# Attention's product with V in single precision, two heads on the two column halves

## The chip, the cores and the metric

The kernel runs on one core of one Trainium2 chip. The metric is the device time of one execution in microseconds (us). Lower is better.

## The reference: what is computed

A trunk of two layers works on a residual stream of 512 positions by 1024 features in float32. Each layer is a SwiGLU feed-forward half-step, a mixer of parallel attention heads, a second feed-forward half-step, and a gated input embedding, with layer norms between. The change is in the mixer, which has three kinds of heads of width 64, all causal over 512 positions:

```python
# 4 "nsa" heads share one key and one value head; two maps each here (selected and window),
# plus a third product with 31 compressed keys:
out = gates[..., 0:1] * o_cmp + gates[..., 1:2] * o_slc + gates[..., 2:3] * o_win
# 4 "diff" heads: one map, the difference of two softmaxes
a = p[:, :, 0] - lam * p[:, :, 1];  o = jnp.einsum('bhqk,bkhd->bqhd', a, v)
# 8 "fox" heads: one map with a decay
p = masked_softmax(s, mask);        o = jnp.einsum('bhqk,bkhd->bqhd', p, v)
```

So a layer has 8 + 4 + 4 x 2 = 20 maps that are multiplied with V, and the program has 40.

## The kernel before

**Precision.** The kernel wants more than rounded precision from TensorE. It writes a float32 value as hi + lo, where hi is the value copied by ScalarE into the rounded type `float32r` and lo is the rest, subtracted by VectorE (`hilo`, lines 241 and 242). A product is then three rounded passes: hi by hi, hi by lo, lo by hi. The projections, the feed-forwards and the output projection are all done so, with weights that stream in by DMA and are split by `_split` (hi on ScalarE at line 218, lo at line 219 on VectorE or, for units tagged "P", on GpSimd). A product of two plain float32 tiles also occurs: line 504 (the decay's running sum, `ut` and `fz`) and line 810 (the norm of the diff heads, `osq` and `bd`).

**A head's way through the mixer.** The string `SEQ` (line 36) lists the steps of a layer's mixer. `G` projects a head's queries and keys; `Q` makes the scores and the softmax (`softmax`, lines 722 to 748: TensorE, a maximum on VectorE at line 733, the exponential on ScalarE at line 735, a reciprocal at line 736, a scaling on VectorE at line 743, or for diff heads at line 747). `T` turns the map (`turn`, lines 750 to 763): ten transposes on TensorE (line 757) into three PSUM tiles, each of which is copied as hi by ScalarE and as lo by VectorE into a tile `PT`. `P` multiplies with V (`PV`, line 850). The letters f, d and n name the kind of head, the digit the head, and a or b the map of an nsa head. The steps are issued in the order of `SEQ`, and a scheduler that builds the program then places each engine's instructions by readiness, so the order on an engine is not that of `SEQ` alone. Each engine works its list in order.

**The product with V.** V is split when it is projected (`split_v`, line 464): ScalarE copies hi, VectorE subtracts lo, and the two lie side by side for each head in `VD`, `VN` and `VF`. `pv` (line 765) has two matmuls for each of the four blocks of keys: one with the 128 columns V hi and V lo against P hi, one with the 64 columns V hi against P lo. Because of the causal mask the four blocks have 512, 384, 256 and 128 moving columns. The compressed keys add two matmuls of 512 columns per nsa head (lines 868, 869). `close` (line 792) then adds the lower and upper halves of the result: ScalarE copies one half to `ob` (line 796), VectorE adds the other (line 798) into half of a tile `pair`. After a pair's second head the 128 rows are scaled by the softmax sums (fox and diff, through four transposes at line 804 and line 805), normed (diff), and split into `oT` for the output projection.

The whole product is done head by head, and each head's `P` comes soon after its `T`.

Of the kernel before, what the change touches and what calls it, by code (L numbers as in the profile page):

```python
# [19 lines left out]
F32 = mybir.dt.float32  # L20
# [15 lines left out]
SEQ = """q0 VF dec Gf1 Gf0 cmp Qf0 kk q1 hk0 Tf0 Pf0 Qf1 hk1 Qn0b Qn0a Tf1 hk2 hk3 Tn0a Gf3 hv0 ck Qn1b Qn1a Tn0b hv1 Qn2b cs Pf1 Pn0a hv2 hv3 Gd0 ct cv Tn1a Gf2 Qn2a Pn0b Pn1a Qn3a Qn3b Tn1b Pn1b Tn2b Tn2a Tn3a Qf2 Tn3b Gd1 Tf2 Pn2a Qf3 Qd0 Pn2b Pn3a Pn3b Pf2 Tf3 Gf4 Gd2 Td0 Qd1 Qf4 Pd0 Pf3 Tf4 Gf5 Qf5 Td1 Gd3 Qd2 Pd1 Tf5 Qd3 Gf6 Pf4 Pf5 Td2 Td3 Gf7 X Qf6 Tf6 Qf7 Pd2 Tf7 Pd3 Pf6 Pf7""".split()  # L36
# [131 lines left out]
class _Body:  # L168
# [258 lines left out]
    def mixer(self, l):  # L427
# [36 lines left out]
        def split_v(dst, p):  # L464
            hi = dst[:, :, 0]
            nc.scalar.activation(hi, p, AF.Copy)
            nc.vector.tensor_sub(dst[:, :, 1], p, hi.bitcast(F32))  # L467
# [204 lines left out]
        def cmp_v():  # L672
# [4 lines left out]
            vc = lw([128, 2, 64], "vc", F32R)  # L677
            self.hilo(vc[:, 0], vc[:, 1], p[:, 0:64])
# [30 lines left out]
        def cmp_t():  # L709
# [4 lines left out]
            pc = self.h4(shape=(128, 2, 512), name="pct")  # L714
            self.hilo(pc[:, 0], pc[:, 1], p)
            M["pc"] = pc
# [33 lines left out]
        def turn(P):  # L750

            res = {}
            for bank, blocks in enumerate((((0, 0), (0, 1), (0, 2), (0, 3)), ((1, 1), (1, 2), (1, 3), (3, 3)),
# [6 lines left out]
                d = self.pt4(shape=(128, 2, n), name="PT")  # L760
                self.hilo(d[:, 0], d[:, 1], p[:, 0:n])
# [30 lines left out]
        def close(po, chunk, half):  # L792
            if chunk not in raws:
                open_(chunk)
            b = self.op.tile([128, 512], F32, name="ob", tag="ot")
            nc.scalar.activation(b[0:64], po[64:128], AF.Copy)
            r = raws[chunk]
            nc.vector.tensor_add(r[64 * half:64 * half + 64], po[0:64], b[0:64])
            if half == 0:
                return  # L800
            if chunk >= 2:
                p = self.ps("t")
                for t in range(NT):
                    nc.tensor.transpose(p[:, 128 * t:128 * t + 128], R[chunk][:, t], self.ident)
                nc.vector.tensor_mul(r, r, p)
# [279 lines left out]
```

## Time and profile before

| | |
|---|---|
| three timed runs | 2170.47, 2180.23, 2185.20 us; median 2180.23 us |
| the profiled execution | 2180.97 us, of which 2179.2 us from the first to the last instruction (the span) |
| TensorE busy, share of the span | 98% |
| VectorE, ScalarE, GpSimd busy | 48%, 38%, 7% |
| mixer of layer 1, of layer 2 | about 365 to 660 us, 1450 to 1750 us of the span |

In the views, PE is TensorE's matmuls, PEld its weight loads, DVE is VectorE, ACT ScalarE, POOL GpSimd. A line such as L249 is a line of the kernel; all matmuls go through the helper at L249 and all splits through L241 and L242, so a group is told by the names of its tiles (`ps<-PT,VF` is a product of a turned map with the fox values). A matmul's duration includes its way through the array, so that durations of neighbours overlap; the pace is read from starts.

### The profile page before, as it was taken

What the parts mean: (1) busy time and instruction counts of PE and PEld (TensorE: products, weight loads), DVE (VectorE), ACT (ScalarE), POOL (GpSimd) and SP (SyncE); (2) the same over time, 40 slices, a digit from 0 to 9 for tenths busy, and PEclk for the clock granted to TensorE, in tenths of its full rate; (3) what the DMA queues carried; (4) which work ended last, traced back from release to release, by engine and by line L of the source; (5) the groups of instructions that cost most, each with busy time, mean ns of one, the idle gap of its engine ahead of it and who ended that gap; (6) DMA issues with size and microseconds to landing.
All of it is one profiled execution on the core that took longest, in us unless ns stands there. A gap on an engine that the chain in (4) does not pass through costs nothing.

```text
span 2179.2 us, 25953 instructions
## 1 busy us (share of the span) xinstructions
PE 2133.2 (98%) x10135; PEld 1771.0 (81%) x10135; DVE 1050.9 (48%) x1777; ACT 819.9 (38%) x1372; POOL 151.7 (7%) x114
## 2 busy tenths in 40 slices
PE   9999999999999999999999999999998999999999
PEld 7888888787778888888888888887877788888887
DVE  4333236378875333335733333363788753333355
ACT  5222214356753222223422222143577532222132
POOL 0000001211210000000000000012212100000000
PEclk9999999999999999999999999999899999999999
DMA  6333334443342333334313333343323413333341
GB/s 202 97 97 97 107 111 147 127 129 94 105 140 63 98 99 97 117 99 136 97 58 97 97 97 106 107 161 119 122 93 110 146 55 97 97 97 116 98 135 68
DMA packets 76107, 236.07 MB, mean 108 GB/s; under 512 B 11344, under 2 KB 13520, under 8 KB 75984
## 3 DMA queue, kind: packets, MB, share of 16 engines
q1 hardware_dynamic: 74864, 230.74, 33.7%
q0 software_dynamic: 1120, 3.67, 0.4%
q8 instruction: 80, 1.31, 0.2%
q14 instruction: 43, 0.35, 0.0%
HBM read 209.46 MB, written 6.29 MB: 99 GB/s over the span
## 4 chain that ended last, share of the span: by engine, by line
PE 88%; DVE 7%; ACT 2%; DMA 2%; issue 1%; SPq 0%; DVEq 0%; ACTq 0%
PE ps L249 85%; PE ps L757 2%; DMA raw<-in_ws_dram 1%; PE ps L266 1%; DVE P L747 1%; ACT whi L218 1%; DVE PT L242 1%; DVE wlo L219 1%; DVE P L733 1%; DVE P L743 0%; DVE raw_r L543 0%; DVE x L303 0%; DVE gy L645 0%; DVE raw_r L541 0%; DMA xraw<-in_xt_dram 0%
## 5 line engine op out<-in xcount | busy, mean ns | idle before, releaser
L218 ACT ACTIVATE whi<-raw 128x1024 fp32r<-128x1024 f32 x342 | 361.7, 1060 | 1039.8 <-PE ps L249 670.5
L219 DVE TENSOR_TENSOR wlo<-raw,whi 128x1024 fp32r<-128x1024 f32 x298 | 364.0, 1224 | 605.0 <-ACT whi L218 604.6
L249 PE MATMUL ps<-xh,wlo 128*128 128x512 f32 (+1 forms) x1688 | 645.1, 382 | 0.2 <-DVE wlo L219 0.2
L249 PE MATMUL ps<-xl,whi 128*128 128x512 f32 (+1 forms) x1688 | 645.0, 382 | 0.0
L249 PE MATMUL ps<-xh,whi 128*128 128x512 f32 (+1 forms) x1688 | 643.9, 382 | 0.8 <-ACT xh L268 0.8
L249 PE MATMUL ps<-whi,h 128*128 128x512 f32 x1376 | 427.2, 389 | 0.0
L249 PEld LDWEIGHTS ps<-xh,whi 128*128 128x128 f32 x1688 | 317.5, 189 | 60.7 <-ACT xh L268 1.5
L249 PEld LDWEIGHTS ps<-xh,wlo 128*128 128x128 f32 x1688 | 318.6, 189 | 58.4 <-DVE wlo L219 0.6
L249 PEld LDWEIGHTS ps<-xl,whi 128*128 128x128 f32 x1688 | 318.3, 189 | 58.2 <-DVE xl L269 0.6
L249 PEld LDWEIGHTS ps<-whi,h 128*128 128x128 f32 x1376 | 258.0, 188 | 53.4
L249 PE MATMUL ps<-wlo,h 128*128 128x512 f32 x704 | 274.1, 389 | 0.0
L335 DVE TENSOR_TENSOR hraw<-silu,ps 128x512 f32<-128x512 f32 x88 | 60.5, 688 | 290.8 <-PE ps L249 290.0
L249 PEld LDWEIGHTS ps<-wlo,h 128*128 128x128 f32 x704 | 132.2, 188 | 27.2
L219 POOL TENSOR_TENSOR wlo<-raw,whi 128x1024 fp32r<-128x1024 f32 x44 | 106.5, 2420 | 291.9 <-ACT whi L218 214.7
L735 ACT ACTIVATE P<-P,sst 128x128 f32<-128x128 f32 x192 | 106.7, 559 | 27.6 <-DVE sst L733 26.9
L249 PE MATMUL ps<-whi,xh 128*128 128x512 f32 (+2 forms) x264 | 100.1, 381 | 4.4 <-DVE VF L467 4.4
L733 DVE CUSTOM_DVE_ANT_0 P<-ps,mask 128x128 f32<-128x128 f32 x192 | 90.4, 491 | 23.7 <-PE ps L249 22.6
L249 PE MATMUL ps<-whi,xl 128*128 128x512 f32 (+2 forms) x264 | 99.8, 379 | 0.0
L298 POOL TENSOR_TENSOR mv<-mv,mhalf 128x1 f32<-128x1 f32 x24 | 23.0, 958 | 1101.4 <-DVE mv L297 1101.4
L249 PE MATMUL ps<-wlo,xh 128*128 128x512 f32 (+2 forms) x264 | 99.7, 379 | 0.0
L757 PE MATMUL ps<-ident,P 128*128 128x128 f32 x400 | 72.1, 300 | 13.0 <-DVE P L747 9.5
L249 PE MATMUL ps<-whi,oT 128*128 128x512 f32 x256 | 82.6, 395 | 0.0
(194 smaller groups left out, 1933.0 us busy)
## 6 DMA issues: line engine op xcount, KB each, us to landing
raw<-in_ws_dram SPq DMA_DIRECT2D x342, 512.0 KB
wraw<-in_ws_dram SPq DMA_DIRECT2D x16, 512.0 KB
dx<-x SPq DMA_DIRECT2D x8, 512.0 KB
x<-dx SPq DMA_DIRECT2D x8, 512.0 KB
rot<-raw_r SPq DMA_DIRECT2D x28, 128.0 KB
bc<-in_ln_g_dram SPq DMA_DIRECT2D x6, 512.0 KB
bc<-in_ln_b_dram SPq DMA_DIRECT2D x6, 512.0 KB
xraw<-in_xt_dram SPq DMA_DIRECT2D x8, 256.0 KB
```

What stands on the lines that cost most here:

```text
L218: self.nc.scalar.activation(hi, r, AF.Copy)
L219: (self.nc.gpsimd if self.opt["pool"] and tag[1:] else self.nc.vector).tensor_sub(lo, r, hi.bitcast(F32))
L242: nc.vector.tensor_sub(lo, src, hi.bitcast(F32))
L249: self.nc.tensor.matmul(out, l, r, start=start, stop=stop, skip_group_check=loose)
L266: nc.tensor.transpose(p[:, j], self.x[t][:, 128 * k:128 * k + 128], self.ident)
L298: nc.gpsimd.tensor_tensor(mv[:, 3:4], mv[:, 2:3], self.mhalf, op=ALU.pow)
L335: nc.vector.tensor_mul(r[0:n], s[up:up + n], pu[up:up + n])
L733: nc.vector.tensor_tensor_reduce(v, p[:, 0:n], self.mask[:, 512 - n:512], -scale, 3e38, ALU.add, ALU.min, nm[:, t:t + 1])
L735: nc.scalar.activation(v, v, AF.Exp, bias=nm[:, t:t + 1], scale=-1.0, accum_out=sm[:, t:t + 1])
L747: nc.vector.scalar_tensor_tensor(v, v, r[:, t:t + 1], c, op0=ALU.mult, op1=ALU.add)
L757: nc.tensor.transpose(p[:, 128 * i:128 * i + 128], P[:, off[t] + 128 * kb:off[t] + 128 * kb + 128], self.ident)
```

## The change

The product of a map with V is done in float32 on unsplit tiles, and two heads are done together. Nothing is split any more on the way: `V` and the turned map are each one copy out of PSUM. `pv` takes the maps of two heads and, for each block of keys, issues one float32 matmul per head, with 64 weight columns: the even head's result goes to partitions 0 to 63 of the PSUM tile, the odd head's to partitions 64 to 127. The two halves need no adding, so `close` is called once for a pair. The compressed values become a tile of four blocks that is zero outside each head's 32 rows, so that its product reads all 128 rows.

In `SEQ` the `P` steps of even heads are gone (what read "Tf0 Pf0 Qf1" reads "Tf0 Qf1"); the `P` of an odd head now does both. The order of the other steps is as before.

```diff
-        VN = self.h4(shape=(128, NT, 2, 2, 64), name="VN")
-        VD = [self.h4(shape=(128, 2, 4, 2, 64), name="VD") for _ in range(2)]
-        VF = [self.h4(shape=(128, 8, 2, 64), name="VF") for _ in range(NT)]
+        VN = self.h4(F32, (128, NT, 2, 64), name="VN")
+        VD = self.h4(F32, (128, NT, 4, 64), name="VD")
+        VF = [self.h4(F32, (128, 2, 8, 64), name="VF") for _ in range(2)]
...
-            split_v(VD[t // 2][:, t % 2], p[:, 0:256].rearrange("p (h d) -> p h d", d=64))
-            split_v(VN[:, t], p[:, 256:384].rearrange("p (h d) -> p h d", d=64))
+            nc.scalar.activation(VD[:, t], p[:, 0:256].rearrange("p (h d) -> p h d", d=64), AF.Copy)
+            nc.vector.tensor_copy(VN[:, t], p[:, 256:384].rearrange("p (h d) -> p h d", d=64))
...
-                split_v(VF[t], p.rearrange("p (h d) -> p h d", d=64))
+                nc.scalar.activation(VF[t // 2][:, t % 2], p.rearrange("p (h d) -> p h d", d=64), AF.Copy)
...
-            vc = lw([128, 2, 64], "vc", F32R)
-            self.hilo(vc[:, 0], vc[:, 1], p[:, 0:64])
+            vc = lw([128, 4, 64], "vc")
+            nc.gpsimd.memset(vc, 0.0)
+            for h in range(4):
+                o = slice(32 * h, 32 * h + 32)
+                nc.vector.tensor_copy(vc[o, h], p[o, 0:64])
...
-            self.hilo(pc[:, 0], pc[:, 1], p)
+            nc.scalar.activation(pc, p, AF.Copy)
...
+            a, b = self.pt4(F32, name="PT"), self.pt4(F32, (128, 256), name="PT")
...
-                d = self.pt4(shape=(128, 2, n), name="PT")
-                self.hilo(d[:, 0], d[:, 1], p[:, 0:n])
+                d = (a[:, 0:512], a[:, 512:1024], b)[bank]
+                nc.scalar.activation(d, p[:, 0:n], AF.Copy)
...
-        def pv(po, PT, v, first, last):
+        def pv(po, PTs, vs, first, last):
             for kb in range(NT):
-                d, a, n = PT[kb]
-                vk = v(kb)
-                o = slice(512 - n, 512)
-                self.mm(po[:, o], vk.rearrange("p a d -> p (a d)"), d[:, 0, a:a + n], first and kb == 0, False, True)
-                self.mm(po[0:64, o], vk[:, 0], d[:, 1, a:a + n], False, last and kb == NT - 1, True)
+                for j in range(2):
+                    d, a, n = PTs[j][kb]
+                    self.mm(po[64 * j:64 * j + 64, 512 - n:512], vs[j](kb), d[:, a:a + n],
+                            first and kb == 0, last and kb == NT - 1, True)
...
-        def close(po, chunk, half):
-            if chunk not in raws:
-                open_(chunk)
-            b = self.op.tile([128, 512], F32, name="ob", tag="ot")
-            nc.scalar.activation(b[0:64], po[64:128], AF.Copy)
+        def close(po, chunk):
+            oT[chunk] = self.h4(shape=(128, 2, 512), name="oT")
+            hi, lo = oT[chunk][:, 0], oT[chunk][:, 1]
+            if chunk < 2:
+                self.hilo(hi, lo, po)
+                return
             r = raws[chunk]
-            nc.vector.tensor_add(r[64 * half:64 * half + 64], po[0:64], b[0:64])
-            if half == 0:
-                return
+            nc.scalar.activation(r, po, AF.Copy)
...
-                o = slice(32 * h, 32 * h + 32)
-                self.mm(p, M["vc"][o].rearrange("p a d -> p (a d)"), M["pc"][o, 0], False, False, True)
-                self.mm(p[0:64], M["vc"][o, 0], M["pc"][o, 1], False, True, True)
-                close(p, h // 2, h % 2)
+                for j, i in enumerate(hs):
+                    self.mm(p[64 * j:64 * j + 64], M["vc"][:, i], M["pc"], False, True, True)
+                close(p, h // 2)
```

The first place is TensorE's list at the first fox head of layer 1, before. PT_3099, PT_3107 and PT_3113 are the three parts of that head's turned map; xs and wraw belong to the compression of the nsa keys, ident and P to the next map's transposes.

```order
L249 MATMUL ps_3116<-PT_3099,VF_2463 128x512
L249 MATMUL ps_3140<-fa_2877,fb_2878 128x384
L249 MATMUL ps_3145<-fb_2878,fa_2877 128x512
L249 MATMUL ps_3145<-fa_2877,fb_2878 128x512
L249 MATMUL ps_3083<-xs_2959,wraw_2996 128x32
L249 MATMUL ps_3116<-PT_3099,VF_2463 64x512
L249 MATMUL ps_3116<-PT_3107,VF_2464 128x384
L249 MATMUL ps_3083<-xs_2959,wraw_2996 128x32 x4
L757 MATMUL ps_3218<-ident_81,P_3128 128x128
```

The same product in the changed kernel, for the first two fox heads, whose maps are PT_3079 and PT_3187:

```order
L249 MATMUL ps_3463<-PT_3079,VF_2462 64x512
L756 MATMUL ps_3242<-ident_81,P_3159 128x128 x2
L756 MATMUL ps_3248<-ident_81,P_3159 128x128
L756 MATMUL ps_3242<-ident_81,P_3159 128x128
L756 MATMUL ps_3248<-ident_81,P_3159 128x128
L756 MATMUL ps_3254<-ident_81,P_3159 128x128
L756 MATMUL ps_3242<-ident_81,P_3159 128x128
L756 MATMUL ps_3248<-ident_81,P_3159 128x128 x2
L756 MATMUL ps_3254<-ident_81,P_3159 128x128
L249 MATMUL ps_3463<-PT_3187,VF_2462 64x512
L249 MATMUL ps_3463<-PT_3079,VF_2462 64x384
L249 MATMUL ps_3335<-nk_3016,nq_2676 128x384
```

The two heads' matmuls of 512 columns are apart here, with ten transposes between them; the odd head's 512 and the even head's 384 are neighbours. The product begins after the second head's map is turned, where before the first head's began at once.

The second place is the last fox pair of layer 1 on TensorE, in the changed kernel. PT_4727 and PT_4728 are one head, PT_4769 and PT_4770 the other.

```order
L249 MATMUL ps_4813<-PT_4769,VF_2462 64x512
L249 MATMUL ps_4813<-PT_4727,VF_2462 64x384
L249 MATMUL ps_4813<-PT_4769,VF_2462 64x384
L249 MATMUL ps_4813<-PT_4728,VF_2463 64x256
L249 MATMUL ps_4813<-PT_4770,VF_2463 64x256
L249 MATMUL ps_4813<-PT_4727,VF_2463 64x128
L249 MATMUL ps_4813<-PT_4769,VF_2463 64x128
```

Here seven of the pair's eight matmuls follow each other, with the heads alternating.

The third place is VectorE at the last diff head of layer 1: the reciprocal of its second softmax and the four combining steps, before.

```order
L242 TENSOR_TENSOR PT_4807<-ps_4802,PT_4807 128x512
L242 TENSOR_TENSOR PT_4815<-ps_4810,PT_4815 128x512
L736 RECIPROCAL sst_4705<-sst_4705 128x4
L242 TENSOR_TENSOR PT_4821<-ps_4818,PT_4821 128x256
L836 SCALAR_TENSOR_TENSOR sst_4705<-sst_4705,nlam_2613,sst_4685 128x4
L242 TENSOR_TENSOR fa_4877<-ps_4852,fa_4877 128x512
L747 SCALAR_TENSOR_TENSOR P_4704<-P_4704,sst_4705,P_4684 128x128
```

And in the changed kernel:

```order
L731 ISA P_4533,sst_4534<-ps_4547,mask_85 128x512
L731 ISA sst_4534 128x1
L734 RECIPROCAL sst_4534<-sst_4534 128x4
L832 SCALAR_TENSOR_TENSOR sst_4534<-sst_4534,nlam_2602,sst_4514 128x4
L745 SCALAR_TENSOR_TENSOR P_4533<-P_4533,sst_4534,P_4513 128x128
```

The three subtractions of a turned map are gone from in front of the combining steps, and the subtraction for `fa` has moved behind them.

## Rows read from the trace of the kernel before

**Rows 1.** The page's first part: busy time of each engine over the span.

```profile
span 2179.2 us, 25953 instructions
PE 2133.2 (98%) x10135; PEld 1771.0 (81%) x10135; DVE 1050.9 (48%) x1777; ACT 819.9 (38%) x1372; POOL 151.7 (7%) x114
```

**Rows 2.** The page's chain of work that ended last, by engine.

```profile
PE 88%; DVE 7%; ACT 2%; DMA 2%; issue 1%; SPq 0%; DVEq 0%; ACTq 0%
```

**Rows 3.** Busy time by stretch: the mixer of layer 1.

```profile
core 0: us, PE busy (x) PEld busy (x) DVE busy (x) ACT busy (x) POOL busy (x), PEclk, DMA share, GB/s
401.40:404.80 3.40, 3.40 (x10) 2.63 (x9) 0.00 (x0) 0.00 (x0) 0.00 (x0) 0.50 0.24 93
404.80:440.00 35.20, 35.20 (x156) 27.58 (x155) 9.15 (x20) 13.69 (x25) 7.16 (x3) 1.00 0.34 99
...
483.30:580.00 96.70, 92.03 (x519) 74.21 (x518) 83.56 (x232) 67.54 (x166) 22.74 (x15) 1.00 0.32 93
580.00:620.00 40.00, 32.99 (x154) 25.36 (x153) 32.75 (x90) 29.81 (x76) 6.70 (x6) 0.87 0.40 128
...
sum 295.00, PE 276.73 PEld 227.81 DVE 212.27 ACT 175.17 POOL 65.16; mean PE 34.59 PEld 28.48 DVE 26.53 ACT 21.90 POOL 8.14
```

**Rows 4.** The same view of the mixer of layer 2, its sum.

```profile
sum 300.00, PE 281.79 PEld 232.94 DVE 216.62 ACT 176.72 POOL 65.40; mean PE 40.26 PEld 33.28 DVE 30.95 ACT 25.25 POOL 9.34
```

**Rows 5.** The span and TensorE's mean granted clock, as a share of full speed.

```profile
core 0: 2179.2 us, clock 0.988
```

**Rows 6.** TensorE's longest waits: line, releaser, us in total, times, longest.

```profile
PE ps L249 <- DVE sst L733: 9.7, 8, 2.4
PE ps L757 <- DVE P L747: 9.5, 7, 2.1
PE ps L249 <- DVE VF L467: 4.4, 2, 2.2
PE ps L757 <- ACT P L735: 3.2, 4, 1.5
```

**Rows 7.** TensorE's instructions in order of time: rounded passes of 512 columns.

```profile
382.30 0.39 PE L249 MATMUL ps<-xl,whi 128*128 128x512 f32 x1
...
387.29 0.39 PE L249 MATMUL ps<-xh,wlo 128*128 128x512 f32 x1
```

**Rows 8.** The same view: one fox head's product with V.

```profile
577.46 1.45 PE L249 MATMUL ps<-PT,VF 128*128 128x512 f32 x8 [0.24 <-DVE pair L798]
```

**Rows 9.** The same view: the plain float32 product of the decay, and the next matmul.

```profile
413.51 2.32 PE L249 MATMUL ps<-ut,fz 128*8 128x512 f32 x8
415.76 0.50 PE L249 MATMUL ps<-xh,whi 128*128 128x512 f32 x1
```

**Rows 10.** Groups by shape: us busy, mean ns, idle before. Work that goes.

```profile
L242 DVE TENSOR_TENSOR PT<-ps,PT 128x512 fp32r<-128x512 f32 x80 | 52.9, 682 | 13.6 <-ACT PT L241 13.2
L798 DVE TENSOR_TENSOR pair<-ps,ob 64x512 f32<-64x512 f32 x32 | 21.8, 680 | 4.8 <-ACT ob L796 4.4
L796 ACT ACTIVATE ob<-ps 64x512 f32<-64x512 f32 x32 | 19.0, 595 | 13.4 <-PE ps L249 13.0
L242 DVE TENSOR_TENSOR PT<-ps,PT 128x256 fp32r<-128x256 f32 x40 | 16.5, 413 | 0.0
L467 DVE TENSOR_TENSOR VF<-ps,VF 128x512 fp32r<-128x512 f32 x8 | 5.3, 689 | 26.5 <-ACT VF L466 26.5
```

**Rows 11.** VectorE in order of time at the last diff head of layer 1.

```profile
606.25 1.28 DVE L242 TENSOR_TENSOR PT<-ps,PT 128x512 fp32r<-128x512 f32 x2
607.45 0.17 DVE L736 RECIPROCAL sst<-sst 128x4 f32<-128x4 f32 x1
...
608.58 4.01 DVE L747 SCALAR_TENSOR_TENSOR P<-P,sst 128x128 f32<-128x128 f32 x4
```

**Rows 12.** ScalarE in order of time at the same place.

```profile
607.00 0.19 ACT L735 ACTIVATION_READ_ACCUMULATOR P<-P,sst 128x1 f32 x1
```

**Rows 13.** TensorE at the same place.

```profile
611.46 1.80 PE L757 MATMUL ps<-ident,P 128*128 128x128 f32 x8 [2.09 <-DVE P L747]
```

More of the change, by code (lines that the diff above doesn't have):

```diff
@@ L34 @@
 NCMP = (S - 32) // 16 + 1
-SEQ = """q0 VF dec Gf1 Gf0 cmp Qf0 kk q1 hk0 Tf0 Pf0 Qf1 hk1 Qn0b Qn0a Tf1 hk2 hk3 Tn0a Gf3 hv0 ck Qn1b Qn1a Tn0b hv1 Qn2b cs Pf1 Pn0a hv2 hv3 Gd0 ct cv Tn1a Gf2 Qn2a Pn0b Pn1a Qn3a Qn3b Tn1b Pn1b Tn2b Tn2a Tn3a Qf2 Tn3b Gd1 Tf2 Pn2a Qf3 Qd0 Pn2b Pn3a Pn3b Pf2 Tf3 Gf4 Gd2 Td0 Qd1 Qf4 Pd0 Pf3 Tf4 Gf5 Qf5 Td1 Gd3 Qd2 Pd1 Tf5 Qd3 Gf6 Pf4 Pf5 Td2 Td3 Gf7 X Qf6 Tf6 Qf7 Pd2 Tf7 Pd3 Pf6 Pf7""".split()
+SEQ = """q0 VF dec Gf1 Gf0 cmp Qf0 kk q1 hk0 Tf0 Qf1 hk1 Qn0b Qn0a Tf1 hk2 hk3 Tn0a Gf3 hv0 ck Qn1b Qn1a Tn0b hv1 Qn2b cs Pf1 hv2 hv3 Gd0 ct cv Tn1a Gf2 Qn2a Pn1a Qn3a Qn3b Tn1b Pn1b Tn2b Tn2a Tn3a Qf2 Tn3b Gd1 Tf2 Qf3 Qd0 Pn3a Pn3b Tf3 Gf4 Gd2 Td0 Qd1 Qf4 Pf3 Tf4 Gf5 Qf5 Td1 Gd3 Qd2 Pd1 Tf5 Qd3 Gf6 Pf5 Td2 Td3 Gf7 X Qf6 Tf6 Qf7 Tf7 Pd3 Pf7""".split()
 def chunks():
@@ L713, in cmp_t @@
                 nc.tensor.transpose(p[:, 128 * t:128 * t + 128], s[:, t].rearrange("p h c -> p (h c)"), self.ident)
-            pc = self.h4(shape=(128, 2, 512), name="pct")
-            self.hilo(pc[:, 0], pc[:, 1], p)
-            M["pc"] = pc
+            pc = M["pc"] = self.h4(F32, (128, 512), name="pct")
+            nc.scalar.activation(pc, p, AF.Copy)
         off = [0, 128, 384, 768]
@@ L790, in later @@
             return w
-        def close(po, chunk, half):
-            if chunk not in raws:
-                open_(chunk)
-            b = self.op.tile([128, 512], F32, name="ob", tag="ot")
-            nc.scalar.activation(b[0:64], po[64:128], AF.Copy)
-            r = raws[chunk]
-            nc.vector.tensor_add(r[64 * half:64 * half + 64], po[0:64], b[0:64])
-            if half == 0:
-                return
[L801 to L805, printed above, removed]
+        def close(po, chunk):
[4 more added lines that the diff above has]
+                return
+            r = raws[chunk]
+            nc.scalar.activation(r, po, AF.Copy)
+            p = self.ps("t")
+            for t in range(NT):
+                nc.tensor.transpose(p[:, 128 * t:128 * t + 128], R[chunk][:, t], self.ident)
+            nc.vector.tensor_mul(r, r, p)
             if chunk in (2, 3):
@@ L813, in close @@
                 nc.vector.scalar_tensor_tensor(r, r, gcol, q, op0=ALU.mult, op1=ALU.mult)
-            oT[chunk] = self.h4(shape=(128, 2, 512), name="oT")
-            self.hilo(oT[chunk][:, 0], oT[chunk][:, 1], r)
+            self.hilo(hi, lo, r)
         Ps, PTs, po = {}, {}, {}
@@ L851, in PV @@
             kind, h = n[0], int(n[1])
-            PT = PTs.pop(n)
+            hs = h - 1, h
+            PT = [PTs.pop(kind + str(i) + n[2:]) for i in hs]
             if kind == "f":
                 p = self.ps("o")
-                pv(p, PT, lambda kb: VF[kb][:, h], True, True)
-                close(p, 4 + h // 2, h % 2)
+                pv(p, PT, [lambda kb, i=i: VF[kb // 2][:, kb % 2, i] for i in hs], True, True)
+                close(p, 4 + h // 2)
             elif kind == "d":
                 p = self.ps("o")
-                pv(p, PT, lambda kb: VD[kb // 2][:, kb % 2, h], True, True)
-                close(p, 2 + h // 2, h % 2)
+                pv(p, PT, [lambda kb, i=i: VD[:, kb, i] for i in hs], True, True)
+                close(p, 2 + h // 2)
             elif n[2] == "a":
                 p = po[h] = self.ps("o")
-                pv(p, PT, lambda kb: VN[:, kb, 0], True, False)
+                pv(p, PT, [lambda kb: VN[:, kb, 0]] * 2, True, False)
             else:
                 p = po[h]
-                pv(p, PT, lambda kb: VN[:, kb, 1], False, False)
-                o = slice(32 * h, 32 * h + 32)
-                self.mm(p, M["vc"][o].rearrange("p a d -> p (a d)"), M["pc"][o, 0], False, False, True)
-                self.mm(p[0:64], M["vc"][o, 0], M["pc"][o, 1], False, True, True)
-                close(p, h // 2, h % 2)
+                pv(p, PT, [lambda kb: VN[:, kb, 1]] * 2, False, False)
+                for j, i in enumerate(hs):
+                    self.mm(p[64 * j:64 * j + 64], M["vc"][:, i], M["pc"], False, True, True)
+                close(p, h // 2)
         def G(n):
```

4 lines of the change are left out of this document (removed).

## Prediction

> **What bounds the kernel now.** I began with the busy times of the page: TensorE works in 98% of the span, VectorE in 48% [rows 1]. The chain of work that ended last says the same, with 88% on TensorE and 7% on VectorE [rows 2]. So a microsecond added to TensorE's list is paid almost in full, and a microsecond taken from VectorE is worth something only where TensorE waits for it. The shares are means over the whole program, so I next looked at the mixer by stretches, where the change is [rows 3]. There the picture differs: between 483 and 580 us VectorE is busy for 83.6 of 96.7 us, and between 580 and 620 us, where TensorE has 33.0 us of work in 40, VectorE has 32.8. TensorE stands idle for 295.0 - 276.7 = 18.3 us in the mixer of layer 1, and for 300.0 - 281.8 = 18.2 us in that of layer 2 [rows 3, 4], together 36.5 us. The reader is to see there too that the granted clock drops to its lower level (1.2 GHz) in some stretches, as 401.4 to 404.8 us, just after the longest wait for the fox values, of 2.2 us [rows 3, 6]. Over the program the mean granted clock is 0.988 of full [rows 5]; the missing 0.012 of 2179 us is 26 us. So 36.5 + 26 = 62.5 us is the most that a mixer without waits could give back. The list of waits says who holds TensorE: nearly always VectorE, with the scores' maximum (9.7 us), the combining and scaling of diff maps (9.5 us) and the fox values (4.4 us) in front [rows 6].
>
> **The base.** The profiled execution took 2180.97 us, 1.8 us more than its span and 0.7 us from the median of the timed runs; I count from 2181.
>
> **Rounded passes removed.** Twenty-two starts lie between 382.30 and 387.29 us, so a rounded pass of 512 columns is paced at 4.99 / 22 = 0.227 us, 0.443 ns a column [rows 7]. A map's product has two passes each of 512, 384, 256 and 128 columns, 2560 in all, which makes 1.13 us; the row of one head's eight matmuls has 1.45 us [rows 8], of which 0.39 - 0.227 = 0.16 us is the last one's way through the array [rows 7]. I take 1.2 us a map, between 1.13 and 1.45 - 0.16 = 1.29. Forty maps are 48 us, and the sixteen matmuls with compressed keys 16 x 0.227 = 3.6 us: 51.6 us go.
>
> **Plain float32 added.** The decay's product is the row to price it by: the code issues four matmuls of 512, 384, 256 and 128 columns, exactly one map's blocks, and the trace has eight. So each float32 matmul is two passes, and the eight take 2.32 us at full clock, 2.16 us without the last one's 0.16 us; the next matmul starts 2.25 us after the first [rows 3, 9]. That is 0.844 ns a column, 1.9 times the rounded pace. The number of columns is the same as before. If every pass has the array to itself, forty maps take 40 x 2.16 = 86.4 us and the compressed keys, eight products of two 512-column passes, 6.9 us: 93.3 us, which is 41.7 us more than what goes.
>
> **What the halves give back.** A map's product now uses 64 weight columns, and the other head's has the other 64. No row of this case has two matmuls on different halves, so this is bounded: nothing at the least; at the most, passes of opposite halves that stand next to each other run together. The even head's two passes need the same half, so what can pair is the second pass of one matmul with the first of the next. I counted such neighbours in TensorE's order of the changed kernel: 102 in the program, 42 of them paired at 128 columns, 30 at 256, 28 at 384 and 2 at 512, 24,832 columns, and at 0.844 ns 21.0 us. If no other instruction stood between, it would be 40 us; but the first fox pair is torn apart by transposes and score matmuls, as the first place shows, while the last pair of the layer is nearly whole. I take the full 21.0 us, because nothing in the two instructions is shared: other weights, other moving tile, other PSUM partitions. That leaves +20.7 us on TensorE, with +41.7 us as the other end.
> The Trainium skill, "TensorE: Matmul & The Clock Gate", in the section on packing small matmuls, gives 2.38 times for three column tiles at once; no run here shows it.
> There could be a price for changing the array's shape. Before, every product with V already alternates 128 and 64 weight columns, and its eight matmuls take 1.45 us where columns and one way through explain 1.29 [rows 8]; at most 0.16 us is left for seven changes and the first weight load. So I add nothing.
> Against that, the Trainium skill, "TensorEngine Tiling (Array Packing)", Key Properties, says that a change of tiling mode drains the engine. A drain priced as one way through, 0.16 us, at both ends of the 66 runs of half-array matmuls would be 21 us more; the row above does not show such drains.
>
> **What VectorE and ScalarE are rid of.** The lo parts of the turned maps (52.9 + 16.5 us), the adding of halves (21.8 us) and the fox values' lo (5.3 us) leave VectorE: 96.5 us [rows 10], out of 212.3 + 216.6 us in the two mixers [rows 3, 4], so 22%. ScalarE loses the 32 copies of a half (19.0 us) and gets 12 copies of a pair's result, at the same 0.595 us 7.1 us [rows 10]. The added memset and small copies for the compressed values come twice in the program and lie beside other work; I put them at nothing, and at under 1 us if they are in the way.
>
> **How much of the waiting goes with it.** Three waits can be followed. At the last diff head the combining begins at 608.58 us, behind three subtractions of a turned map and one for `fa`, while ScalarE's last sum was there at 607.19 [rows 11, 12]. In the new order these stand elsewhere (the third place), so it can begin after the reciprocal and one small step, near 607.6: 1.0 us of TensorE's wait of 2.09 us [rows 13]. What is late next is ScalarE's exponential, and the combining itself with 4.01 us. The fox values' wait of 2.2 us ends with a subtraction of 0.69 us [rows 6, 10], so a third of it goes. The longest waits for a maximum, 2.4 us each, are VectorE stuck in the chain for compressed keys, which stays. So between nothing and half of each; I take 40% of the 62.5 us, clock included, which is 25 us. Bounds: 0, if the chains of softmax set the waits; 47 us (75%), if a VectorE that is free a fifth more of the time is hardly ever late.
> A new wait could come from the pair: its product waits for the second head's map. But the first head's map is no longer needed by anyone, and the queue behind the product is that of other heads, so nothing is added for it.
>
> **Sum.** 2181 + 41.7 - 21.0 - 25.0 = 2176.7, so 2177 us: 0.2% less, which is no change. About 1% (21.8 us, so 2159 and 2203 us) is what a measurement of this kernel can tell from none.
>
> **Rivals.**
> *VectorE was the real limit of the mixer.* The halves run together and three quarters of the waits go: 2181 + 20.7 - 47 = 2155 us. For it speaks VectorE's 86% between 483 and 580 us [rows 3] and that VectorE is named in the longest waits; against it the chain of the last diff head, where only 1.0 of 2.09 us could go.
> *The halves do not run together.* TensorE takes each pass alone, as it takes all matmuls of the trace one after the other. Then 2181 + 41.7 - 25 = 2198 us, slower than before. It decides against the change as soon as the waits give back less than 42 us, and costs over 1% if they give back under 20. For it speaks that the whole trace shows no two matmuls side by side, only weight loads beside a matmul (1771 us of PEld beside 2133 us of PE [rows 1]); against it that the instructions share nothing.
> *The clock falls in the new products.* Should each of the 20 pair products bring one stretch at the lower level as long as that at 401.4 us, 3.4 us with half of it lost, it is 34 us on the forecast: 2211 us. Against it: the decay's product fills only 8 weight columns for 2.3 us, and the clock stays full up to 440 us [rows 3, 9].
>
> **Chances and range.** The forecast has 0.45, VectorE as the limit 0.22, halves apart 0.27, the clock 0.06. Faster by over 1%: 0.18 of the second and 0.03 of the forecast's upper end, 0.21. Slower by over 1%: 0.11 of the third, 0.06 of the fourth and 0.01 of the forecast, 0.18. Within: 0.61. The forecast's own range is 2162 to 2196 us (40% of the waits becoming 64% or 10%). The whole range goes down to 2148, a little beyond the second case, and up to 2206, halves apart with 17 us given back.
>
> **What would show it.** In the changed profile, matmuls named `ps<-PT,VF` should be 64 columns wide and come twice per product. If halves run together, an alternating run such as the last fox pair's should have starts at about half of 0.43 us for 512 columns, that is the odd head's first pass starting with the even head's second; if not, starts are a full pass apart and TensorE's busy time in each mixer is about 21 us up, not 10. VectorE's busy time in a mixer should be near 164 us. TensorE's waits for VectorE should fall from 9.7 + 9.5 + 4.4 = 23.6 us on the three longest rows [rows 6] to some 14, and the mean clock rise to 0.993. The prediction is wrong if the waits stay as they are or vanish, or if the clock's mean falls below 0.98.

## The result and the profile after

The changed kernel takes 2190.52 us (median of 12 runs, 2187.9 to 2194.3), the kernel before 2173.85 us in the same comparison: ratio 1.0085, 95% interval 1.0068 to 1.0102. So it is a little slower, by 0.85%. One of the twelve executions of before took 4280.69 us and stands outside the ratio. The forecast was 2177 us, no change, in a range of 2148 to 2206 us. The profiled execution of after took 2188.26 us, 7.3 us more than that of before (2180.97); between the medians it is 16.7 us.

The page's first part, of after:

```profile
span 2186.5 us, 25714 instructions
PE 2154.5 (99%) x10135; PEld 1748.5 (80%) x10135; DVE 942.8 (43%) x1613; ACT 804.9 (37%) x1342; POOL 152.1 (7%) x116
```

Against [rows 1], TensorE's busy time is up by 21.3 us, VectorE's down by 108 us, and the time in which TensorE does nothing falls from 46.0 to 32.0 us. 21.3 - 14.0 is the 7.3 us of the two spans. The chain of work that ended last has gone over to TensorE still more [rows 2]:

```profile
PE 91%; DVE 4%; ACT 2%; DMA 2%; issue 1%; SPq 0%; DVEq 0%; ACTq 0%
```

Over the timed executions the granted clock did not rise: its mean is 0.990 in the 59 of before that stand beside the experiments, and 0.989 in the 17 of the changed kernel. Between the two profiled executions it rose by 0.002 [rows 5]; span and mean clock of after:

```profile
core 0: 2186.5 us, clock 0.990
```

Busy time by stretch in the mixer of layer 1 (columns as in [rows 3]):

```profile
401.40:404.80 3.40, 3.40 (x16) 2.82 (x15) 0.00 (x0) 0.00 (x0) 0.00 (x0) 1.00 0.41 159
...
445.00:483.00 38.00, 36.03 (x203) 31.10 (x201) 24.73 (x74) 20.48 (x59) 8.32 (x5) 0.82 0.38 129
483.00:580.00 97.00, 96.92 (x512) 67.50 (x510) 53.80 (x181) 62.91 (x159) 20.86 (x16) 1.00 0.30 88
580.00:620.00 40.00, 34.03 (x151) 22.46 (x150) 24.77 (x72) 26.88 (x68) 7.34 (x6) 0.89 0.30 93
...
sum 300.00, PE 287.73 PEld 217.65 DVE 158.42 ACT 167.72 POOL 65.04; mean PE 41.10 PEld 31.09 DVE 22.63 ACT 23.96 POOL 9.29
```

Between 483 and 580 us VectorE went from 83.6 to 53.8 us of work and TensorE from 92.0 to 96.9 of 97: TensorE waits for nobody there now, and a further microsecond saved on VectorE there is worth nothing. Idle time in this mixer fell from 18.3 to 300 - 287.7 = 12.3 us. TensorE's longest waits, against [rows 6]:

```profile
PE ps L756 <- ACT P L733: 4.9, 2, 2.4
PE ps L249 <- ACT VF L479: 4.6, 2, 2.3
PE ps L756 <- DVE P L745: 4.5, 3, 2.2
PE ps L756 <- DVE P L741: 3.0, 2, 2.0
...
PE ps L249 <- DVE sst L731: 0.4, 2, 0.2
```

VectorE's 9.7 us for the scores' maximum are 0.4 (L731 now), its 9.5 for combining the diff maps 4.5 (L745 now); 3.0 for the scaling of the other maps (L741) are new; the fox values' wait is as long as before (4.6 for 4.4 us), and ScalarE's copy ends it now.

The products themselves, TensorE's instructions in order of time (start, us to the modelled end, x counts passes, two for each matmul):

```profile
531.87 1.07 PE L249 MATMUL ps<-PT,VN 128*64 128x512 f32 x2
532.87 0.44 PE L249 MATMUL ps<-fb,fa 128*128 128x384 f32 x1
...
533.89 1.07 PE L249 MATMUL ps<-PT,VN 128*64 128x512 f32 x4
534.89 0.33 PE L249 MATMUL ps<-dk,dq 96*128 96x128 f32 x1
535.15 0.86 PE L249 MATMUL ps<-PT,VN 128*64 128x384 f32 x4
```

Here are both things that I had to guess. One head's matmul of 512 columns takes 1.00 us from its start to the next matmul's; two heads' (x4, one head's 512 columns beside the other's 384) take 1.00 us as well. So the halves run together wholly, not only in neighbouring passes. But two passes at 0.844 ns a column [rows 9] are 0.86 us, and the next full-array matmul starts 0.14 us later than that: the run pays something beside its passes. In TensorE's list the products of the program lie in 66 such runs, parted by other matmuls. By the order of the list and 0.83 ns a column and pass, the longer half of each run sums to 64.0 us; the forecast had 72.3 (93.3 - 21.0).

### The profile page after: what moved, and what is told of

It reads as the page before. It is cut to its first block, busy times and chain, and to the rows that moved or that the text cites. A ratio compares the mean times of both kernels' runs of the same rounds, so it can differ in the third digit from the quotient of the medians.

```text
span 2186.5 us, 25714 instructions
## 1 busy us (share of the span) xinstructions
PE 2154.5 (99%) x10135; PEld 1748.5 (80%) x10135; DVE 942.8 (43%) x1613; ACT 804.9 (37%) x1342; POOL 152.1 (7%) x116
## 4 chain that ended last, share of the span: by engine, by line
PE 91%; DVE 4%; ACT 2%; DMA 2%; issue 1%; SPq 0%; DVEq 0%; ACTq 0%
PE ps L249 88%; PE ps L756 2%; DMA raw<-in_ws_dram 1%; PE ps L266 1%; DVE wlo L219 1%; ACT P L733 1%; ACT whi L218 0%; DVE P L741 0%; DVE x L303 0%; DMA rot<-raw_r 0%; DVE rot L537 0%; PE ps L801 0%; DVE P L745 0%; DVE raw_r L538 0%; DVE xl L269 0%
## 5 line engine op out<-in xcount | busy, mean ns | idle before, releaser
L249 PEld LDWEIGHTS ps<-wlo,h 128*128 128x128 f32 x704 | 132.1, 188 | 27.5
L731 DVE CUSTOM_DVE_ANT_0 P<-ps,mask 128x128 f32<-128x128 f32 x192 | 87.8, 487 | 77.1 <-PE ps L249 56.6
L733 ACT ACTIVATE P<-P,sst 128x128 f32<-128x128 f32 x192 | 106.4, 558 | 25.9 <-DVE sst L731 25.3
L756 PE MATMUL ps<-ident,P 128*128 128x128 f32 x400 | 65.4, 291 | 12.8 <-ACT P L733 4.9
```

Of the source, the lines that this page charges most:

```text
L249: self.nc.tensor.matmul(out, l, r, start=start, stop=stop, skip_group_check=loose)
L731: nc.vector.tensor_tensor_reduce(v, p[:, 0:n], self.mask[:, 512 - n:512], -scale, 3e38, ALU.add, ALU.min, nm[:, t:t + 1])
L733: nc.scalar.activation(v, v, AF.Exp, bias=nm[:, t:t + 1], scale=-1.0, accum_out=sm[:, t:t + 1])
L756: nc.tensor.transpose(p[:, 128 * i:128 * i + 128], P[:, off[t] + 128 * kb:off[t] + 128 * kb + 128], self.ident)
```

## The experiments

Five theories. A: each run of half-array matmuls pays about 0.24 us for going in and coming out (0.14 as above, some 0.1 from the starts ahead of a run), 16 us in all. B: changing the shape costs nothing, only overlap counts. C: the halves give back next to nothing. D: the late place of the even head's product costs by itself. E: VectorE's relief is worth little. In the table the kernel before is 2172 to 2177 us, and the clock is the profiled execution's mean.

| kernel | median us | ratio to before, 95% | clock |
|---|---|---|---|
| changed kernel, again | 2190.12 | 1.0073, 1.0047 to 1.0098 | 0.989 |
| uninterrupted runs | 2172.95 | 0.9997, 0.9980 to 1.0014 | 0.987 |
| halves in turn | 2194.49 | 1.0106, 1.0075 to 1.0137 | 0.989 |
| full width | 2186.58 | 1.0072, 1.0045 to 1.0098 | 0.993 |
| order alone (rounded) | 2205.31 | 1.0139, 1.0100 to 1.0177 | 0.979 |
| heads apart, early | 2203.90 | 1.0117, 1.0095 to 1.0139 | 0.994 |
| heads apart, late | 2231.39 | 1.0261, 1.0228 to 1.0294 | 0.987 |
| lo parts kept | 2184.54 | 1.0034, 1.0017 to 1.0050 | 0.989 |
| filler kernel | 2159.54 | 0.9911, 0.9888 to 0.9934 | 0.992 |
| filler kernel, again | 2161.89 | 0.9917, 0.9901 to 0.9933 | 0.991 |
| filler, zeros ahead | 2176.96 | 1.0005, 0.9989 to 1.0021 | 0.987 |
| filler, zeros between | 2193.44 | 1.0084, 1.0059 to 1.0110 | 0.987 |
| filler, lo parts kept | 2190.15 | 1.0057, 1.0036 to 1.0077 | 0.987 |
| filler, products later | 2185.25 | 1.0028, 1.0014 to 1.0043 | 0.984 |

### Uninterrupted runs, and the halves in turn

The first matmul of a product waits for all six parts of the two turned maps, and all eight are set ahead of other work, so that nothing stands between them:

```diff
+            with self.tc.high_priority():
+                m0 = None
                 for kb in range(NT):
                     for j in range(2):
...
+                        if m0 is None:
+                            m0 = m
+                            for P in PTs:
+                                for c in P[4]:
+                                    self.tc.add_manual_dep(m.ins, c.ins.name, mybir.DependencyInfo(
+                                        mybir.DependencyClass.Sync, mybir.DependencyReason.DATA), reason="all turned")
```

> The changed kernel, with each pair's eight (or ten) half-array matmuls made one uninterrupted run in TensorE's order: 20 runs in place of 66, and the longer of the two halves streams 46.1 us in all at full clock in place of 64.0 (worked out from the order and 0.83 ns a column and pass). The arithmetic is the same. Theory A (each run of half-array matmuls pays about 0.24 us for going in and coming out): 17.9 us of streaming and 46 x 0.24 = 11 us of changing go, 29 us, about 2162 us, ratio to the kernel before about 0.994. Rival B (changing the shape costs nothing, only the overlap counts): 18 us go, about 2173 us, ratio 1.000. Rival C (the halves give back next to nothing, the rest is float32's own pace): about 2190 us, ratio 1.008, as the changed kernel. A wait for the pair's last turned map, which now holds the product's first matmul, could take back a few microseconds under each.

17 us came back, the figure of B, where A had 29. But the trace does not read as B: from each product's start to the next other matmul the products take 51.0 us in place of 76.3 (summed over the 336 passes), 25.3 us less where B has 17.9, and the rest of TensorE's list takes 11.5 us more, by idle time and by the clock (0.990 to 0.987). C falls. In the second kernel the two loops are exchanged, so that the even head's four matmuls stand ahead of the odd head's:

```diff
-                for kb in range(NT):
-                    for j in range(2):
+                for j in range(2):
+                    for kb in range(NT):
```

> As the kernel with uninterrupted runs (20 of them), but inside a run the even head's matmuls all stand ahead of the odd head's, so that the halves can overlap only where the one list ends and the other begins. Same arithmetic, same number of changes of the array's shape. Theory A with halves that overlap only as far as the engine takes matmuls in order: streaming about 88 us in place of 46, so 42 us more than the uninterrupted run, about 2204 us. Rival B (no price for changing): the same 42 us between the two, so this run sizes the overlap alone. Rival C (halves give nothing): no difference between the two. If each half had a queue of its own, eight matmuls deep, the difference would be nothing as well, and the starts in the trace would show it.

It lost 21.5 us against the other, where A and B both had 42. The products took 81.0 us in place of 51.0, and the rest of the list 11.2 us less. One product, in order of time:

```profile
528.66 3.93 PE L249 MATMUL ps<-PT,VN 128*64 128x512 f32 x16
532.51 0.44 PE L249 MATMUL ps<-fb,fa 128*128 128x384 f32 x1
```

3.85 us, where the two heads woven take 2.30 (below) and two heads one after the other would take twice 2.16 and 0.14, 4.46. So the overlap depends on the order of issue, but a little of the second list slips under the end of the first: 0.6 us, for twenty products 12 us of the 42.

### Full width

The weight tiles get 64 columns of zeros beside them and are 128 wide; both heads add into all rows of the result.

```diff
-                    self.mm(po[64 * j:64 * j + 64, 512 - n:512], vs[j](kb), d[:, a:a + n],
-                            first and kb == 0, last and kb == NT - 1, True)
+                    self.mm(po[:, 512 - n:512], vs[j](kb).rearrange("p a d -> p (a d)"), d[:, a:a + n],
+                            first and kb == 0 and j == 0, last and kb == NT - 1 and j == 1, True)
```

> The changed kernel with each weight tile of 64 columns widened with 64 columns of zeros to 128, so that every product with V uses the full array and both heads add into all 128 rows of the result; it computes the same. No change of the array's shape is left (0 runs of half-array matmuls) and no overlap: streaming 92.2 us at full clock in place of 64.0. Theory A (0.24 us a run): +28.2 of streaming, - 66 x 0.24 = -16: 12 us above the changed kernel, about 2203 us, ratio 1.013. Rival B (changing costs nothing): +28 us, about 2219 us, ratio 1.021. Rival C (halves give nothing): about 2190 us, 1.008, or under.

Better than under A or B, and within what C had, which has fallen above: with 28 us more to stream it is no slower than the changed kernel. Its page has

```profile
PE 2161.2 (99%) x10135; PEld 1776.8 (81%) x10135; DVE 951.3 (44%) x1621; ACT 805.2 (37%) x1342; POOL 157.0 (7%) x132
```

6.7 us more of TensorE than after. As the clock took some 6 us less (0.993 for 0.990), that is about 13 us at full clock; A says 12, B 28. Idle time (25.5 us of the span for 32.0) and the clock give it back. So the trace speaks for A, though the time does not show it. One product of two heads at full width, in order of time:

```profile
501.02 0.28 PE L249 MATMUL ps<-nkl,nq 128*128 128x256 f32 x1
501.14 4.48 PE L249 MATMUL ps<-PT,VN 128*128 128x512 f32 x16
505.45 0.60 PE L761 MATMUL ps<-ident,P 128*128 128x128 f32 x4
```

4.31 us, twice 2.16 and nothing over. So float32 passes at full width pay no gap among other full-array matmuls; the 0.14 us belong to the half-array runs.

### The zeros: the price of changing the shape

This pair settles it. It is built on the filler kernel below. Sixty rounded matmuls with zeros, 128 columns wide, are added; in the one they stand together ahead of the product, in the other they cut it in four.

```diff
                 for k in range(1, 2 * NT):
                     one(k // 2, k % 2)
+                    if k in (1, 3, 5):
+                        self.mm(po[:, 384:512], zz, zz, False, False, True)
```

> The filler kernel (20 uninterrupted runs) with work added: three rounded matmuls with zeros, 128 weight columns and 128 moving columns, stand straight ahead of each pair's product, 60 in the program; they add zeros and change no result. The number of runs of half-array matmuls stays 20. It is the control for the kernel with the zeros in between. Each zero matmul at 0.057 us or a little more (128 of the 0.443 ns columns): about 3.5 us above the filler kernel's 2160, so 2163 us, ratio 0.993, under every theory.

> The same 60 matmuls with zeros as in the control, now one after the first, the second and the third pair of half-array matmuls of each product: 80 runs of half-array matmuls in place of 20, with the same streaming (46.1 us), because every pair of equal length stays whole. Theory A (0.24 us a run for going in and out): 60 x 0.24 = 14.4 us above the control, about 2177 us. Rival B (changing the array's shape costs nothing; what the uninterrupted runs won was all overlap): the same as the control within 3 us, about 2163 us. In the trace a product with zeros in between should take 2.30 + 3 x (0.24 + 0.057) = 3.2 us under A and 2.5 us under B.

TensorE in order of time, zeros ahead:

```profile
529.00 0.45 PE L249 MATMUL ps<-zz 128*128 128x128 f32 x3
529.38 2.37 PE L249 MATMUL ps<-PT,VN 128*64 128x512 f32 x16
531.68 0.44 PE L249 MATMUL ps<-fb,fa 128*128 128x384 f32 x1
```

and zeros between:

```profile
531.45 1.08 PE L249 MATMUL ps<-PT,VN 128*64 128x512 f32 x4
532.46 0.33 PE L249 MATMUL ps<-zz 128*128 128x128 f32 x1
532.71 0.87 PE L249 MATMUL ps<-PT,VN 128*64 128x384 f32 x4
533.51 0.33 PE L249 MATMUL ps<-zz 128*128 128x128 f32 x1
533.77 0.65 PE L249 MATMUL ps<-PT,VN 128*64 128x256 f32 x4
534.35 0.33 PE L249 MATMUL ps<-zz 128*128 128x128 f32 x1
534.61 0.44 PE L249 MATMUL ps<-PT,VN 128*64 128x128 f32 x4
534.98 0.45 PE L249 MATMUL ps<-fb,fa 128*128 128x384 f32 x1
```

The same work takes 531.68 - 529.00 = 2.68 us together and 534.98 - 531.45 = 3.53 us cut up: 0.85 us for three more changes there and back, 0.28 us each. Over all twenty products, the products and the zeros together take 76.8 us in place of 61.2, 0.26 us for each of the 60; but for the zeros, TensorE's two lists agree in all but 4 of 10,135 places. The whole programs, on one chip, differ by 16.5 us for 60, 0.27 us each (by the two intervals 0.18 to 0.39). A holds, B falls. The 66 runs of the changed kernel pay 66 x 0.28 = 18.5 us. The Trainium skill, "TensorEngine Tiling (Array Packing)", Key Properties, says that a change of tiling mode drains the engine: these rows agree, with 0.28 us for there and back.

The control missed: 2177 us where I expected 2163. The zeros' rows are 8.5 us of it, start to next start; for the rest I have only that TensorE's list around them was laid anew (some 150 places differ from the filler kernel's) and the mean clock fell from 0.992 to 0.987. So between kernels with different lists some ten microseconds say nothing by themselves.

### The place of the products

First the order alone, in the kernel before with its rounded passes. Of the hand-written list (two of the places):

```diff
-Tf0 Pf0 Qf1
+Tf0 Qf1
...
-cs Pf1 Pn0a hv2
+cs Pf0 Pf1 hv2
```

> The kernel before with its rounded passes, in which only the hand-written order of steps is changed: the even head's product with V stands next to the odd head's, where the changed kernel does the pair. Nothing of the arithmetic changes. Under theory A and rival B the order alone is worth nothing that can be told: 2174 us within 5, ratio 0.998 to 1.002. If the later products are what costs (a rival D: the first head's work comes late and its filling is missing in the waits), it is slower by 8 us or more, ratio over 1.004.

Slower by 33 us between the medians (22 to 38 by the interval): D, and far more than I thought. Between the profiled executions it is 24.1 us, of which TensorE's clock has 2203.3 us of span x (0.988 - 0.979) = 20 us and idle time 3.4 us. Its longest wait is one that the list of before does not have:

```profile
PE ps L757 <- DVE PT L242: 6.7, 6, 2.3
```

These are transposes that wait for VectorE's lo part of a turned map. A late product also holds the tiles of its turned map for longer, and their pool has six (tag "p"), three for a rounded map and two for a float32 one. So D has two readings, the filling that a wait has lost and a pool that is full, and no run parts them. Then in float32, first at the early places and without pairing:

```diff
+            e = h % 2
+            o = slice(64 * e, 64 * e + 64)
             if kind == "f":
                 p = self.ps("o")
+                pv(p[o], PT, lambda kb: VF[kb // 2][:, kb % 2, h], True, True)
+                close(p[o], 4 + h // 2, e)
```

> The changed kernel without its pairing: plain float32 on the head's own half of the array, but each head's product at the place in the order that it had in the kernel before, so that the halves never run together (70 runs of half-array matmuls, 92.2 us of streaming in place of 64.0). It computes the same. Theory A alone (streaming and 0.24 us a run, places in the order worth nothing): 28 + 1 us above the changed kernel, about 2219 us, ratio 1.021. Theory A with rival D (the even head's late product costs what the kernel before lost when its order alone was changed, 33 us): those 33 us come back, about 2186 us, ratio 1.006. In between, the difference to 2219 is what the early places are worth in the float32 kernel.

> The kernel with float32 heads apart, with the even head's product moved to its late place beside the odd head's, as in the changed kernel and as in the run that changed the order alone; each head's matmuls still stand by themselves in the code (78 runs, 90.5 us of streaming, against 70 and 92.2). It computes the same. Rival D (late products cost by themselves, 33 us with rounded passes): 15 to 33 us above the 2204 us of the early places, ratio 1.018 to 1.027. If the late place is free where turned maps are one float32 tile in place of two rounded ones: within 5 us of 2204, ratio 1.010 to 1.014.

The early places gave 2203.9, between the two expectations; the late ones 2231.4, 27.5 us more (1.4%, 31 us, by the ratios, as the two had different executions of before beside them). The mean clock is 0.994 and 0.987, and idle time 24.1 and 33.0 us. Here a single head's product has its half to itself:

```profile
505.39 2.37 PE L249 MATMUL ps<-PT,VN 128*64 128x512 f32 x8
507.69 0.77 PE L756 MATMUL ps<-ident,P 128*128 128x128 f32 x5
```

2.30 us for one head.

### The filler kernel

The first matmul of a product keeps its ordinary place in the order; only the other seven follow at once.

```diff
-            with self.tc.high_priority():
-                m0 = None
...
+            m = one(0, 0)
...
+            with self.tc.high_priority():
+                for k in range(1, 2 * NT):
+                    one(k // 2, k % 2)
```

> As the kernel with uninterrupted runs (20 runs, 46.1 us of streaming, same arithmetic), but the first matmul of a product has its ordinary place in the order, not one ahead of all else, and only the other seven follow it at once. In the kernel with uninterrupted runs, the products took 25.3 us less than in the changed kernel but the rest took 11.5 us more, in idle time and at the lower clock. If that came from products that run at the first moment and then lack as filling in a wait, some of it returns here: 2160 to 2168 us, ratio 0.994 to 0.998. If it is the price of less work in the mixer whatever its place (the chains of softmax set the time), it stays at 2170 to 2175 us, ratio 0.999 to 1.001.

2159.5 us, and 2161.9 on another chip: faster than before by 0.9%, than the changed kernel by 1.3 to 1.7%. One pair in order of time:

```profile
532.74 2.37 PE L249 MATMUL ps<-PT,VN 128*64 128x512 f32 x16
535.04 0.44 PE L249 MATMUL ps<-fb,fa 128*128 128x384 f32 x1
```

2.30 us for two heads, the same as for the single head above: the second head is free. The clock is back at 0.992.

> The filler kernel once more, nothing edited, with more rounds: the base for the two beside it and the version that is faster than both kernels. 2155 to 2165 us, ratio 0.988 to 0.994.

> The filler kernel with every pair's product written up to two steps later in the hand-written order, so that in TensorE's list five of the ten products of a layer stand 2 to 60 instructions later and one earlier. Same arithmetic, 20 runs. If a product is worth more the later it stands (as filling, as the step from the first moment to the ordinary place gave 13 us): under the filler kernel by 2 to 8 us, ratio 0.987 to 0.990. If late products cost by themselves, as with heads apart: 5 to 20 us above it, ratio 0.993 to 1.001.

23 us slower than the filler kernel on the same chip, with the clock at 0.984: from the ordinary place on, later is worse. So neither the first moment nor the latest is best. What exactly a late product leaves uncovered I have not isolated; the clock carries (0.991 - 0.984) x 2187 = 15 us of it.

### VectorE's relief

The lo part of each turned map is still made, into tiles that nothing reads:

```diff
+                nc.vector.tensor_sub(los[bank], p[:, 0:n], d)
```

> The changed kernel, in which VectorE still makes the lo part of every turned map (120 subtractions, as before the change) into tiles that nothing reads. TensorE's work is the same as in the changed kernel, and its runs 60 in place of 66. It sizes what VectorE's relief gave. My forecast's theory (VectorE holds TensorE; 25 us came from the relief): most of it lost, 12 to 20 us above the changed kernel, 2202 to 2210 us, ratio about 1.015. Rival E (the waits are set by the chains of softmax, and VectorE's spare time is worth little): under 5 us, 2188 to 2195 us, ratio 1.007 to 1.010.

No loss at all: 2184.5 us, even 6 us less than the changed kernel, which its 60 runs and 61.0 us of streaming nearly explain (3.0 + 6 x 0.28 = 4.7). So in the changed kernel the relief is worth nothing that can be told: E. (Some 600 of the 10,135 places in TensorE's list differ from the changed kernel's, so a few microseconds either way stay open.) The same in the filler kernel:

> The filler kernel, in which VectorE still makes the lo part of every turned map (120 subtractions into tiles that nothing reads). The products take TensorE 27 us less than in the changed kernel, so VectorE's relief could count here even though it did not there. Rival E (VectorE's spare time is worth little): within 6 us of the filler kernel, ratio 0.989 to 0.996. My forecast's theory (VectorE holds TensorE as soon as TensorE is quick enough): 12 us or more above it, ratio over 0.997.

28 us lost. TensorE's longest waits there, first of the filler kernel on that chip, then with the lo parts kept:

```profile
PE ps L249 <- ACT VF L479: 5.8, 2, 3.1
PE ps L712 <- DVE sc L705: 5.5, 2, 2.7
PE ps L249 <- DVE g L647: 3.0, 2, 1.7
```

```profile
PE ps L712 <- DVE gy L640: 10.9, 2, 5.4
PE ps L759 <- DVE P L745: 10.2, 6, 3.7
PE ps L759 <- ACT P L733: 5.7, 4, 2.4
```

And 300 us of the mixer of layer 1, in the same order:

```profile
365.00:665.00 300.00, 287.73 (x1526) 226.81 (x1526) 174.53 (x448) 174.41 (x391) 67.34 (x46) 0.97 0.40 123
```

```profile
365.00:665.00 300.00, 276.10 (x1434) 216.32 (x1433) 193.41 (x482) 168.06 (x380) 66.03 (x45) 0.95 0.38 121
```

With 19 us more of VectorE's work TensorE does 12 us less in the same stretch, and over the program its idle time goes from 33.6 to 56.4 us. I read it so: VectorE holds TensorE where TensorE's own list is short, and not where it is long. Some 600 places of the list differ here too, so a part of the 28 us may be order.

The changed kernel once more, on the chip of the zeros and of the late heads:

> The changed kernel once more, nothing edited, on the chip of these runs: 2185 to 2195 us, ratio 1.006 to 1.011. Under every theory; it tells how far the ratios of this kernel differ from chip to chip, and gives a second profile.

2190.1 us, as the first time.

## Why the prediction was wrong

A step put at nothing was not nothing, the clock gave nothing back, and other errors hid part of it.

**"So I add nothing" (changing the array's shape).** This is the first step that failed: 0.28 us for each of the 66 runs, 18.5 us. I read the price off the alternation of 128 and 64 columns in [rows 8], which shows no such gap; it doesn't stand for a run of float32 passes on a half (why rounded passes of 64 columns pay nothing, no run takes up). And I passed over the row that shows a part of it: in [rows 9], behind a float32 product of 8 weight columns, the next full-array matmul starts 2.25 us after the first, 0.09 us past the 2.16 that I counted. The price I had set beside it (21 us) was the right size.

**"So nothing is added for it" (the product waits for the second head's map).** I asked who is queued behind the product, not what the even head's product did at its early place, nor what its tiles hold up when it comes late. Moving it late costs 33 us in the rounded kernel and 27.5 us in float32 with heads apart, more of it by the clock than by idle time. In the changed kernel it can't be undone alone, since the pair needs both maps. So it is shown that the step is unsafe, and not shown what it cost here.

**"102 opposite-half neighbours", 21.0 us.** Too small, and the picture of it wrong: the halves are served side by side for a whole run, as 1.00 us for one head and for two shows. The overlap is 92.2 - 64.0 = 28.2 us, and 46 us where runs are whole, more than the 40 that I gave as its most. That the torn runs lose part of it was right.

**Rounded passes, 51.6 us.** From the starts in the trace of before, waits left out, the products took 76.9 - 14.3 = 62.6 us, 6.1 us of it at the lower clock, so 59.6 us at full clock. I had priced them at the pace of an unbroken row, 8 us short. So the terms on TensorE come to 64.0 + 18.5 - 59.6 = 22.9 us at full clock, and the forecast had +20.7: by luck nearly a right sum of wrong terms. The page has +21.3, and some 25 at full clock, as the clock took 4 us less in this execution.

**The waits, 25 us.** They were 14.6 us of idle time and 10.4 us of clock. The idle time fell by 14.0 us, VectorE's time in the mixer of layer 1 to 158.4 us (164 forecast), and the three rows' 23.6 us to 9.5 (0.4 + 4.5 + 4.6; some 14 forecast), beside the new 3.0. The clock is the second step that failed: it rose to 0.990, not 0.993, in the profiles, which is 4 us, and over the timed executions it did not rise at all (0.990 before, 0.989 after), so that of the 10.4 us nothing came back. And the reason fails: with VectorE's work put back the kernel takes no longer. What covered the waits instead is open; kernels whose products take longer (full width, heads apart early) have less idle time, which fits a longer list on TensorE that fills its own gaps, but no run takes that alone.

**The base.** I counted from the profiled 2181 us, "0.7 us from the median of the timed runs". Over 12 runs that median is 2173.85. The profiled execution of after is 11.6 us over the forecast's 2176.7: 6 by the clock, 5 by TensorE's time at full clock, under 1 by idle time. That makes the change 7.3 us from profile to profile; the other 9 of the 16.7 us between the medians are the base, an execution of before that was 7 us longer than its median and one of after that was 2 us shorter. Some 4 of these 7 us are that execution's clock, 0.988 where the mean is 0.990. Span times clock, which leaves the clock out, is 11 us longer in the profiles and 12 us over all executions. So of the 21 us between the forecast's change (4 us down) and the measured one (17 us up), I estimate about 13 for the clock and 5 for TensorE's list.

Of the rivals, "the halves do not run together" had the nearest number (2198 us) with a mechanism that the rows refute, "VectorE was the real limit" is borne out only in the filler kernel, and the 34 us of the clock's fall did not come: 4.7 us of the new products stood at the lower level, 10.5 in the second profile of the changed kernel, for 6.1 before.

## What to carry to other kernels

Small matmuls on parts of the array pay off in unbroken runs: bring all parts' operands together first, weave the parts matmul by matmul, let nothing else between, and count the runs in the engine's list at 0.28 us each (measured for float32 halves among rounded full-array matmuls) before forecasting a gain. Making two products into one moves the first of them to the time of the second; price that too: late places cost 27 to 33 us in two kernels here, the clock having the larger part. And relief of an engine is worth what the other engine then waits for it: nothing where the other is busy 97 of 97 us, up to 28 us once its own list is shorter.

## What the runs showed of the hardware

- A pair of float32 products on opposite halves, eight passes each, takes 2.30 us, and one such product alone 2.30 us.
- A run of float32 passes on the halves takes 0.14 us beside its passes until the next full-array matmul starts (1.00 for 0.86, 2.30 for 2.16); with what its neighbours lose, there and back costs 0.28 us. Float32 at full width has no such gap (4.31 us for two heads), nor have the rounded passes of before that alternate 128 and 64 columns [rows 8].
- With one half's whole list ahead of the other's, a pair takes 3.85 us, 0.6 us less than one after the other.
- The placing of the same products in TensorE's list moved the mean clock by 0.007 (heads apart; filler) to 0.009 (rounded passes), 15 to 20 us, as much as all the changes of shape.
